# The second projection's weights and the samples' operands prepared in small steps, one or two between the products of a part

## The chip, the core and the metric

The kernel runs on one core of a Trainium2 chip. The core has a matrix engine (TensorE, PE in the profile), a vector engine (VectorE, DVE), a scalar engine (ScalarE, ACT), a general engine (GpSimd, POOL) and a sequencer that issues most of the transfers (SyncE, SP); 16 DMA engines carry them. The metric is the time of one execution on the device in microseconds (us), the median of several runs.

## The reference, cut to what matters

The kernel computes one layer of a streaming encoder: a recurrent and an attention mixer, a cross-attention into a memory, and a feed-forward block, for 1024 prompt rows and for 128 sample rows (8 requests of 16). Only the last product and the norm behind it are touched:

```python
def swiglu(x, w_in, w_out):
    g, u = jnp.split(x @ w_in, 2, axis=-1)
    return (jax.nn.silu(g) * u) @ w_out              # w_out: 2816 x 1024, the "second projection"
...
    x = layer_norm(ALPHA * x + swiglu(x, w_ffn_in, w_ffn_out), ln_g[2], ln_b[2])
```

## The kernel before, in words

All matrices are fp32. A product of two fp32 operands is done as three matmuls in a shorter format: each operand is split into a high part (a cast on ACT) and a low part (operand minus high part, a subtraction on DVE or POOL), and `mm3` (line 96) issues high by high, high by low and low by high into one PSUM bank. A matmul of 128x128 by 128x512 is the unit.

The second projection is the last stage, `second_projection`. The 2816 rows of its weights are 22 blocks of 128, taken as 11 *pairs*; each pair, with the two halves of the 1024 columns, is a 2x2 block matrix (a11, a12, a21, a22). A Strassen-like scheme needs seven block products (*steps*) rather than eight; its weight operands are A11, S1, S2, S4, S3, A12, A22 with s1 = a21+a22, s2 = s1−a11, s4 = a12−s2, s3 = a11−a21, and its activation operands B11, T1, T2, B22, T3, B21, T4 come from `h_scratch` in DRAM. The table `steps` lists for each step the PSUM bank (x, z or w, two buffers each), the weight operand, the activation operand and where its result goes.

`PARTS` cuts the 11 pairs into (0,2), (2,4), (4,6), (6,8), (8,11). For each part the seven steps run for row blocks b = 0 and 1, then the samples' product of the part (bank s), then the seven steps for b = 2 and 3. In the first four parts a step of a turn has 12 matmuls, 6 for each b. In the last part there are three pairs and each b runs alone, 9 matmuls a step; its results go through `final_norm` (lines 1083 to 1097), the layer norm: statistics and two multiplies on DVE, `rs` (a power) and two more operations on POOL, one on ACT, and then the stores. The norm of the samples (`ys`) was issued between b = 1 and b = 2.

After a step's matmuls for one b, DVE adds the bank into the accumulator `y` (line 1196; bank w instead is copied by ACT to `tap` and added by POOL, line 1194). Steps S2, S3 and A22 go on accumulating in bank x, and S4 in bank z, so such a step's matmuls wait for the DVE add of the step before in that bank.

`prepare(i)` makes the operands of pair i: two loads of 512 KB into `raw2` (line 1108, SP), four sums on POOL (lines 1111 to 1114), eight casts on ACT (line 1121), six low parts on DVE and two, A21 and A22, on POOL (line 1122). It takes one of 14 buffers ("units") of pool `c` for the sums, four for the results and, for every other pair, one for raw2; the other raw2 is in pool `f2`. `operand()` gives a step its activation operand, loads (line 1164, `hq`) three steps ahead and splits (lines 1173 and 1174, `hh` and `hl`) one step ahead. The order of instructions on each engine comes from a scheduler which starts from the order in which the code issues the work; engines run their own lists in order and wait on semaphores.

Pairs 0 and 1 are prepared in the stage before, and the scheduler moves pair 2 there too. The others are prepared as `more()` is called in the code: one pair of the next part between the first half and the sample's product, the rest after the sample's product; pair 3 is so prepared in part 0.

Of the kernel before, what the change touches and what calls it, by code (L numbers as in the profile page):

```python
# [9 lines left out]
F32 = mybir.dt.float32  # L10
F32R = mybir.dt.float32r
# [3 lines left out]
ALU = mybir.AluOpType  # L15
# [3 lines left out]
P = 128  # L19
# [13 lines left out]
PAIRS = FT // 2  # L33
# [19 lines left out]
class Order:  # L53
# [49 lines left out]
def trunk(ctx, tc, I, O):  # L103
    nc = tc.nc
# [814 lines left out]
    def unit(c, name, dt=F32):  # L919
        return c.tile([P, 2048], dt, name=name, tag="u", bufs=14)  # L920
# [178 lines left out]
    def second_weights(c):  # L1099

        prepared = {}

        def prepare(i, at):

            raw = (at.tile([P, 2, 1024], F32, name="raw2") if at else unit(c, "raw2").rearrange("p (n x) -> p n x", n=2))
            a11, a12, a21, a22 = (raw[:, n, x * 512:x * 512 + 512] for n in range(2) for x in range(2))
            for n in range(2):
                nc.sync.dma_start(out=raw[:, n], in_=I["w_f2"][n, i])
            sums = unit(c, "s2").rearrange("p (n x) -> p n x", x=512)
            s1, s2, s3, s4 = (sums[:, n] for n in range(4))  # L1110
            G.tensor_tensor(s1, a21, a22, op=ALU.add)  # L1111
            G.tensor_tensor(s2, s1, a11, op=ALU.subtract)
            G.tensor_tensor(s4, a12, s2, op=ALU.subtract)
            G.tensor_tensor(s3, a11, a21, op=ALU.subtract)
            out = {}
            for both in ((("A11", a11), ("S1", s1)), (("S2", s2), ("S4", s4)), (("S3", s3), ("A12", a12)),
                         (("A22", a22), ("A21", a21))):
                t = unit(c, "w2", F32R).rearrange("p (n x) -> p n x", x=512)
                for n, (name, src) in enumerate(both):
                    hi, lo = t[:, 2 * n], t[:, 2 * n + 1]  # L1120
                    S.copy(hi, src)  # L1121
                    (G if name in ("A21", "A22") else V).tensor_tensor(lo, src, hi.bitcast(F32), op=ALU.subtract)  # L1122
                    out[name] = hi, lo
            prepared[i] = out
# [12 lines left out]

        return prepared, prepare, first_operands

    def second_projection(f2, c, ahead, prepared, prepare):  # L1140

        y = {}
        sums = [bank("s") for _ in range(2)]
        gb = []
# [54 lines left out]
            if bn is not None:  # L1199
                V.bn_stats(bn[:, half], y[b, e][:, hs])  # L1200

        def blocks(part, bs, gb):

            ws = [prepared[i] for i in range(*part)]
            bk = {}
            bn = {(b, e): sm.tile([P, 2, 6], F32, name="bn", bufs=6) for b in bs for e in range(2)} if gb else {}
            for which, w, h, start, (e, half, fin) in steps:
                for b, hs in zip(bs, ahead.pop((bs[0] + part[0], h), None) or operand()):
                    if start:
                        bk[which, b] = bank(which)  # L1210
                    ps = bk[which, b]
                    for n, wk in enumerate(ws):
                        mm3(ps, hs[n], wk[w], start and n == 0, n == len(ws) - 1, skip_group_check=not start)
                    add(b, e, half, ps, None if fin is None else bn.get((b, fin)), which)
                    if gb and (w == "S3" or w == "A22"):
                        final_norm(y[b, fin], gb, bn[b, fin], b, fin)
                    yield

        def sample_operands(part):
            out = []  # L1220
            for i in range(*part):
                q, hi, lo = (f2.tile([P, 2, P], t, name=x, bufs=2) for x, t in (("hs", F32), ("hsh", F32R), ("hsl", F32R)))
                nc.sync.dma_start(out=q, in_=hs_dram[:, i])
                split(q, hi, lo)
                out.append((hi, lo))
            return out

        def sample(part, hs, first, last):
            ws = [prepared[i] for i in range(*part)]
# [16 lines left out]
        for n, part in enumerate(PARTS):  # L1246
            last = n == len(PARTS) - 1
            if n == 0:
                for e in range(2):
                    for b in range(2):  # L1250
                        nc.sync.dma_start(out=y[b, e], in_=x2_dram[TILES[b + 4 * e]])
            if last:
                both = unit(c, "ln_gb").rearrange("p (n x) -> p n x", n=2)
                gb = [both[:, n] for n in range(2)]
                for n in range(2):
                    nc.sync.dma_start(out=gb[n], in_=I["ln"][4 + n:5 + n, :].broadcast_to([P, D]))
            for bs in ((0,), (1,)) if last else ((0, 1),):
# [24 lines left out]
            yield from blocks(part, (2, 3), gb)  # L1282

    def feed_forward(rows):
        right.close()
        c = ctx.enter_context(tc.tile_pool(name="c", bufs=1, side="right", reuse_waits="tile"))
        ops = {o: tuple(unit(c, f"{o}_{x}", F32R).rearrange("p (k x) -> p k x", k=4) for x in "hl") for o in OPS}
        ready, filled = Event(), Event()
        order.add(all_operands(ops, rows, ready), 6)
        order.add(filler(filled), 10)  # L1290
        yield ready
        yield filled
        prepared, prepare, first_operands = second_weights(c)
        ops2 = {}

        def ahead():
            for i in range(PARTS[0][1]):
                prepare(i, None)
# [193 lines left out]
```

## Time and profile before

| | |
|---|---|
| runs, us | 1694.09 median of 3 (1692.74 to 1698.1) |
| profiled execution, us | 1695.47, its span 1693.6 |
| PE busy | 1618.2 us, 96% of the span |
| DVE, ACT, POOL busy | 1127.7, 677.5, 497.1 us |
| the stage of the change | first y load issued at 1397.6, last instruction 1690.0, end 1693.6 |
| its transfers, from 1395 us on | 40.6 MB |

A PE that is busy is not at its peak; what counts in this stage are the places where PE has nothing to do, or is granted half its clock (PEclk 0.5). One step of 12 matmuls takes 2.81 us when nothing holds it, 0.234 us for each.

### The profile page before, as it was taken

To read this page: it belongs to the slowest core of one execution; us is meant where nothing else is said; L and a number is where in the kernel's file an instruction comes from. 1 tells how busy PE (TensorE), PEld (TensorE's weight loads), DVE (VectorE), ACT (ScalarE), POOL (GpSimd) and SP (SyncE) were. 2 spreads that over 40 slices of the span, in tenths; PEclk is the share of its full clock that TensorE was granted. 3 is DMA by queue.
4 is the path that set the end of the run, shared out by engine and by line. 5 is a ranking of instruction groups with operands and counts; after the bars stand their busy time and mean duration, and the time that the engine had idled before them with its cause. 6 is when DMAs were issued, how large, how long until landed. Compare 5 with 4: busy or idle time off the path is not lost.

```text
span 1693.6 us, 24454 instructions
## 1 busy us (share of the span) xinstructions
PE 1618.2 (96%) x9065; PEld 1392.1 (82%) x9065; DVE 1127.7 (67%) x2025; ACT 677.5 (40%) x1372; POOL 497.1 (29%) x384
## 2 busy tenths in 40 slices
PE   8999999999999999999997999999999997889897
PEld 7998999999888987789895888888888875667675
DVE  6786688778478666787677555444444575675677
ACT  4543556446443545134343333223222343344332
POOL 1111121111000000000056443333332463765665
PEclk9999999999999999999998999999999998999999
DMA  7443343334885589637363222222222137434242
GB/s 242 140 162 123 103 148 104 100 116 127 289 280 170 174 270 307 216 115 258 125 196 104 93 100 93 97 90 97 97 96 97 69 106 245 132 104 137 90 155 87
DMA packets 118951, 247.92 MB, mean 146 GB/s; under 512 B 11952, under 2 KB 63536, under 8 KB 118832
## 3 DMA queue, kind: packets, MB, share of 16 engines
q1 hardware_dynamic: 118832, 246.36, 43.7%
q8 instruction: 71, 1.16, 0.3%
q14 instruction: 48, 0.39, 0.1%
HBM read 203.65 MB, written 42.60 MB: 145 GB/s over the span
## 4 chain that ended last, share of the span: by engine, by line
PE 78%; DVE 7%; DMA 5%; POOL 5%; issue 3%; ACT 2%; SPq 1%; POOLq 0%; ACTq 0%; DVEq 0%
PE a L96 47%; PE b L96 20%; PE x L96 4%; PE b L100 2%; PE z L96 2%; PE s L96 1%; PE w L96 1%; DMA raw<-in_w_f_dram 1%; DMA w_raw<-in_w_f_dram 1%; DVE w L1122 1%; POOL s L1111 1%; DMA w_raw<-in_w_mv_dram 1%; DVE w_lo L137 1%; ACT w L1121 1%; DVE y L1196 1%
## 5 line engine op out<-in xcount | busy, mean ns | idle before, releaser
L137 DVE TENSOR_TENSOR w_lo<-w_raw,w_hi 128x1024 fp32r<-128x1024 f32 (+1 forms) x169 | 205.2, 1217 | 116.7 <-ACT w_hi L136 116.2
L136 ACT CAST w_hi<-w_raw 128x1024 fp32r<-128x1024 f32 (+1 forms) x169 | 174.6, 1035 | 207.2 <-PE a L96 79.6
L96 PE MATMUL a<-w_hi,q_hi 128*128 128x256 f32 (+1 forms) x576 | 196.9, 343 | 0.7 <-ACT kv_sb L270 0.7
L96 PE MATMUL a<-w_lo,q_hi 128*128 128x256 f32 (+1 forms) x576 | 196.5, 341 | 0.0
L96 PE MATMUL a<-w_hi,q_lo 128*128 128x256 f32 (+1 forms) x576 | 195.5, 339 | 0.0
L96 PE MATMUL a<-q_hi,w_hi 128*128 128x384 f32 x528 | 187.0, 354 | 6.7 <-ACT q_hi L136 4.3
L96 PE MATMUL a<-q_hi,w_lo 128*128 128x384 f32 x528 | 180.1, 341 | 0.0
L96 PE MATMUL a<-q_lo,w_hi 128*128 128x384 f32 x528 | 180.0, 341 | 0.0
L96 PE MATMUL x<-w,hh 128*128 128x512 f32 x344 | 112.0, 408 | 31.5 <-DVE y L1196 15.7
L137 DVE TENSOR_TENSOR w_lo<-a,w_hi 128x1024 fp32r<-128x1024 f32 x43 | 73.0, 1698 | 78.5 <-ACT w_hi L136 78.5
L96 PEld LDWEIGHTS a<-w_hi,q_hi 128*128 128x128 f32 x576 | 108.4, 188 | 14.9 <-ACT kv_sb L270 1.1
L96 PEld LDWEIGHTS a<-w_lo,q_hi 128*128 128x128 f32 x576 | 108.6, 189 | 14.2 <-issue 1.2
L96 PEld LDWEIGHTS a<-w_hi,q_lo 128*128 128x128 f32 x576 | 108.4, 188 | 12.5 <-issue 0.4
L96 PEld LDWEIGHTS a<-q_hi,w_hi 128*128 128x128 f32 x528 | 100.6, 191 | 11.9 <-ACT q_hi L136 4.7
L96 PEld LDWEIGHTS x<-w,hh 128*128 128x128 f32 x344 | 65.8, 194 | 51.2 <-ACT hh L1173 16.1
L699 POOL TENSOR_TENSOR rs<-rs,mhalf 128x1 f32<-128x1 f32 x18 | 17.3, 959 | 303.5 <-DVE rs L698 303.5
L96 PE MATMUL a<-T_h,w_hi 128*128 128x512 f32 x264 | 104.7, 396 | 0.0
L96 PE MATMUL a<-T_h,w_lo 128*128 128x512 f32 x264 | 104.6, 396 | 0.0
L96 PE MATMUL a<-T_l,w_hi 128*128 128x512 f32 x264 | 104.6, 396 | 0.0
L96 PEld LDWEIGHTS a<-q_lo,w_hi 128*128 128x128 f32 x528 | 100.8, 191 | 1.9 <-DVE q_lo L137 0.9
L96 PEld LDWEIGHTS a<-q_hi,w_lo 128*128 128x128 f32 x528 | 100.5, 190 | 0.8 <-DVE w_lo L137 0.4
L1173 ACT CAST hh<-hq 128x512 fp32r<-128x512 f32 (+1 forms) x82 | 47.0, 582 | 91.5 <-PE x L96 46.2
(308 smaller groups left out, 3929.9 us busy)
## 6 DMA issues: line engine op xcount, KB each, us to landing
a<-in_w_f_dram SPq DMA_DIRECT2D x44, 512.0 KB, 5.1
w_raw<-in_w_fm_dram SPq DMA_DIRECT2D x41, 512.0 KB, 3.9
h_scratch<-w_raw SPq DMA_DIRECT2D x55, 256.0 KB, 2.2
hq<-h_scratch SPq DMA_DIRECT2D x54, 256.0 KB, 3.9
w_raw<-in_w_tm_dram SPq DMA_DIRECT2D x24, 512.0 KB, 3.4
w_raw<-in_w_out_dram SPq DMA_DIRECT2D x24, 512.0 KB, 5.1
w_raw<-in_w_mq_dram SPq DMA_DIRECT2D x24, 512.0 KB, 4.3
w_raw<-in_w_mo_dram SPq DMA_DIRECT2D x24, 512.0 KB, 4.5
```

Of the source, the lines that this page charges most:

```text
L96: return self.eng.matmul(out, lhsT, rhs, **kw)
L100: return self.eng.transpose(out, in_, identity)
L136: S.copy(hi, src)
L137: V.tensor_tensor(lo, src, hi.bitcast(F32), op=ALU.subtract)
L699: G.tensor_tensor(rs, rs, mhalf[:, 0:1], op=ALU.pow)
L1111: G.tensor_tensor(s1, a21, a22, op=ALU.add)
L1121: S.copy(hi, src)
L1122: (G if name in ("A21", "A22") else V).tensor_tensor(lo, src, hi.bitcast(F32), op=ALU.subtract)
L1173: S.copy(hi, q)
L1196: V.scalar_tensor_tensor(y[b, e][:, hs], y[b, e][:, hs], 1.0 if key in y else ALPHA, ps, op0=ALU.mult, op1=ALU.add)
```

## The change

`prepare` no longer issues anything. It returns a table of small steps: `load`, two `a` (two sums each), four `u` (two casts each) and four `l` (two low parts each). A new function `plans` puts the steps of the next part's pairs, and the loading (`load_sample`) and splitting (`part_sample`) of the samples' operands, into lists, one list for each of the seven steps of the first half and of the second half; `blocks` runs a list after its step. The first of the next part's pairs is planned into the first half, the second (and third) into the second half; the second's load also stands in the first half. The samples' operands get three buffers instead of two. `more()` is gone, and so is the preparation of one pair ahead after the first half: pair 3 is now loaded in part 0, before the second step's operands.

```diff
-            raw = (at.tile([P, 2, 1024], F32, name="raw2") if at else unit(c, "raw2")...)
...
+            raw, sums, units, out = [], [], [], prepared.setdefault(i, {})
+
+            def load():
+                t = at().tile([P, 2, 1024], F32, name="raw2") if at else unit(c, "raw2").rearrange("p (n x) -> p n x", n=2)
+                for n in range(2):
+                    nc.sync.dma_start(out=t[:, n], in_=I["w_f2"][n, i])
...
+            def add(k):
...
+            def upper(k):
...
+                    S.copy(t[:, 2 * n], src)
+
+            def lower(k):
...
+                    (G if name in ("A21", "A22") else V).tensor_tensor(lo, src, hi.bitcast(F32), op=ALU.subtract)
+                    out[name] = hi, lo
+            return {"load": load, **{f"a{k}": (lambda k=k: add(k)) for k in range(2)},
+                    **{f"u{k}": (lambda k=k: upper(k)) for k in range(4)},
+                    **{f"l{k}": (lambda k=k: lower(k)) for k in range(4)}}
...
-        def blocks(part, bs, gb):
+        def blocks(part, bs, gb, plan=()):
...
+                for x in plan[z] if plan else ():
+                    x()
...
-        def more():
-            i = len(prepared)
-            if i < PAIRS:
-                prepare(i, f2 if i % 2 else None)
+        def plans(n, load_sample, part_sample):
+            first, second = [[] for _ in steps], [[] for _ in steps]
+            first[2].append(load_sample)
+            first[5].append(part_sample)
+            if n + 1 < len(PARTS):
+                nexts = [prepare(i, (lambda: f2) if k == 1 else None) for k, i in enumerate(range(*PARTS[n + 1]))]
...
+                put(first, 0, load=0, a0=1, a1=2, u0=2, l0=3, u1=3, l1=4, u2=4, l2=5, u3=5, l3=6)
+                put(first, 1, load=1)
+                put(second, 1, a0=0, a1=0, u0=0, l0=1, u1=1, l1=2, u2=2, l2=3, u3=3, l3=4)
+                if len(nexts) > 2:
+                    put(second, 2, load=3, a0=5, a1=5, u0=5, l0=6, u1=6, l1=6, u2=6, l2=6, u3=6, l3=6)
+            return first, second
...
                 for n in range(2):
                     nc.sync.dma_start(out=gb[n], in_=I["ln"][4 + n:5 + n, :].broadcast_to([P, D]))
+            load_sample, part_sample, hx = sample_operands(part)
+            first, second = plans(n, load_sample, part_sample)
             for bs in ((0,), (1,)) if last else ((0, 1),):
-                yield from blocks(part, bs, gb)
-            hs = sample_operands(part)
+                yield from blocks(part, bs, gb, first if bs[-1] == 1 else ())
...
-            while len(prepared) < min(part[1] + 1, PAIRS):
-                more()
-            yield from sample(part, hs, n == 0, last)
+            yield from sample(part, hx, n == 0, last)
...
-            while len(prepared) < PARTS[n + 1][1]:
-                more()
-            yield from blocks(part, (2, 3), gb)
+            yield from blocks(part, (2, 3), gb, second)
```

One thing the diff does not say aloud: in the last part the loop over `gb` uses the name `n` too and leaves it at 1, so that `plans(n, ...)` there is `plans(1, ...)`. It plans the pairs of `PARTS[2]` once more; the list `first` then runs with block b = 1 of the last part. Pair 4 is prepared a second time in full (two loads, four sums, eight casts, eight low parts) and pair 5 is loaded a second time; nothing reads what they make.

How the instructions stand now, at three places.

SP at the start of the stage: the loads of `y` (the accumulators of b = 0 and 1), then those of `hq` (activation operands from the third step on). Before:

```order
L1251 DMA y_13037<-x2_scratch 128x1024
L1251 DMA y_13040<-x2_scratch 128x1024
L1251 DMA y_13041<-x2_scratch 128x1024
L1164 DMA hq_13080<-h_scratch 128x512
L1164 DMA hq_13082<-h_scratch 128x512
```

and in the changed kernel:

```order
L1295 DMA y_13037<-x2_scratch 128x1024
L1295 DMA y_13040<-x2_scratch 128x1024
L1295 DMA y_13041<-x2_scratch 128x1024
L1110 DMA raw2_13086<-in_w_f2_dram 128x1024 x2
L1184 DMA hq_13089<-h_scratch 128x512
L1184 DMA hq_13091<-h_scratch 128x512
```

Pair 3's two loads (raw2_13086), which stood behind eight `hq` and more, now stand ahead of the first; on ACT two casts of this pair stand ahead of the first `hh`, on POOL its four sums ahead of the first `hl`, and on DVE two of its low parts ahead of the first `hl`.

DVE where part 0 ends and part 1 begins: y_13038 and y_13039 take the last step of b = 2 and 3, y_13036 and y_13037 the first of part 1; raw2, s2 and w2 are here the loaded blocks, the sums and the results of pair 4, the first of part 1. Before:

```order
L1174 TENSOR_TENSOR hl_13489<-hq_13442,hh_13488 128x512
L1196 SCALAR_TENSOR_TENSOR y_13038<-y_13038,x_13298 128x512
L1122 TENSOR_TENSOR w2_13612<-raw2_13604,w2_13612 128x512
L1122 TENSOR_TENSOR w2_13612<-s2_13607,w2_13612 128x512
L1196 SCALAR_TENSOR_TENSOR y_13039<-y_13039,x_13306 128x512
L1122 TENSOR_TENSOR w2_13617<-s2_13607,w2_13617 128x512
L1196 SCALAR_TENSOR_TENSOR y_13036<-y_13036,x_13448 128x512
L1122 TENSOR_TENSOR w2_13617<-s2_13607,w2_13617 128x512
L1196 SCALAR_TENSOR_TENSOR y_13037<-y_13037,x_13456 128x512
```

and in the changed kernel:

```order
L1139 TENSOR_TENSOR w2_13521<-raw2_13464,w2_13521 128x512
L1194 TENSOR_TENSOR hl_13498<-hq_13442,hh_13497 128x512
L1216 SCALAR_TENSOR_TENSOR y_13038<-y_13038,x_13273 128x512
L1139 TENSOR_TENSOR w2_13521<-s2_13489,w2_13521 128x512
L1139 TENSOR_TENSOR w2_13546<-s2_13489,w2_13546 128x512
L1216 SCALAR_TENSOR_TENSOR y_13039<-y_13039,x_13281 128x512
L1139 TENSOR_TENSOR w2_13546<-s2_13489,w2_13546 128x512
L1216 SCALAR_TENSOR_TENSOR y_13036<-y_13036,x_13448 128x512
L1139 TENSOR_TENSOR w2_13571<-s2_13489,w2_13571 128x512
L1216 SCALAR_TENSOR_TENSOR y_13037<-y_13037,x_13456 128x512
```

The A11 low part moved ahead of the add of b = 2, and S2's moved ahead of the add of b = 3, beside S1's; the loads of pair 4, on SP, now stand together (before: one of pair 5, one of pair 4, two `hq`, the other of pair 4).

DVE in the last block, b = 3, of the last part: y_13039 and y_13043 are its accumulators, y_13038 and y_13042 those of b = 2, ys those of the samples; x, z, w and s are the banks. Before:

```order
L1196 SCALAR_TENSOR_TENSOR y_13039<-y_13039,x_15179 128x512
L1083 BN_AGGR mv_15157<-bn_15022 128x2
L1174 TENSOR_TENSOR hl_15241<-hq_15207,hh_15240 128x384
L1084 TENSOR_SCALAR rs_15158<-mv_15157 128x1
L1089 SCALAR_TENSOR_TENSOR y_13038<-y_13038,mv_15157,ln_gb_14646 128x512
L1086 SCALAR_TENSOR_TENSOR nb_15159<-mv_15157,rs_15158 128x1
L1196 SCALAR_TENSOR_TENSOR y_13043<-y_13043,z_15196 128x512
L1090 SCALAR_TENSOR_TENSOR y_13038<-y_13038,rs_15158,ln_gb_14646 128x512
L1196 SCALAR_TENSOR_TENSOR y_13043<-y_13043,x_15179 128x512
L1196 SCALAR_TENSOR_TENSOR y_13043<-y_13043,z_15196 128x512
```

and in the changed kernel:

```order
L1216 SCALAR_TENSOR_TENSOR y_13039<-y_13039,x_15210 128x512
L1194 TENSOR_TENSOR hl_15272<-hq_15238,hh_15271 128x384
L1139 TENSOR_TENSOR w2_14867<-raw2_14817,w2_14867 128x512
L1139 TENSOR_TENSOR w2_14867<-s2_14837,w2_14867 128x512
L1139 TENSOR_TENSOR w2_14889<-s2_14837,w2_14889 128x512 x2
L1139 TENSOR_TENSOR w2_14925<-s2_14837,w2_14925 128x512
L1139 TENSOR_TENSOR w2_14925<-raw2_14817,w2_14925 128x512
L1216 SCALAR_TENSOR_TENSOR y_13043<-y_13043,z_15227 128x512
L1216 SCALAR_TENSOR_TENSOR y_13043<-y_13043,x_15210 128x512
L1216 SCALAR_TENSOR_TENSOR y_13039<-y_13039,w_15304 128x512
L1316 SCALAR_TENSOR_TENSOR ys_15032<-ys_15032,s_13034 128x512
L1316 SCALAR_TENSOR_TENSOR ys_15032<-ys_15032,s_13035 128x512
```

The second preparation's six low parts now stand between the adds of b = 3, and behind them the samples' sums and norm and the norm of b = 2, which stood before b = 3's adds or between them; the last three adds of b = 3 and its two norms come behind those. The load of `ys` on SP takes the buffer of the second preparation's sums (s2_14837), and so comes after the low parts that read them; those sums and results take buffers that the S1 step of b = 3 is the last to read.

More of the change, by code (lines that the diff above doesn't have):

```diff
@@ L1103, in prepare @@
         def prepare(i, at):
[L1105 to L1111, printed above, removed]
@@ new lines, in load @@
+            def load():
+                t = at().tile([P, 2, 1024], F32, name="raw2") if at else unit(c, "raw2").rearrange("p (n x) -> p n x", n=2)
+                for n in range(2):
+                    nc.sync.dma_start(out=t[:, n], in_=I["w_f2"][n, i])
+                raw.extend(t[:, n, x * 512:x * 512 + 512] for n in range(2) for x in range(2))
+            def add(k):
+                a11, a12, a21, a22 = raw
+                if k == 0:
+                    t = unit(c, "s2").rearrange("p (n x) -> p n x", x=512)
+                    sums.extend(t[:, n] for n in range(4))
+                s1, s2, s3, s4 = sums
+                for o, x, y, op in (((s1, a21, a22, ALU.add), (s2, s1, a11, ALU.subtract)),
+                                    ((s4, a12, s2, ALU.subtract), (s3, a11, a21, ALU.subtract)))[k]:
+                    G.tensor_tensor(o, x, y, op=op)
@@ new lines, in names @@
+            def names(k):
+                a11, a12, a21, a22 = raw
+                s1, s2, s3, s4 = sums
+                return ((("A11", a11), ("S1", s1)), (("S2", s2), ("S4", s4)), (("S3", s3), ("A12", a12)),
+                        (("A22", a22), ("A21", a21)))[k]
+            def upper(k):
+                t = unit(c, "w2", F32R).rearrange("p (n x) -> p n x", x=512)
+                units.append(t)
+                for n, (_, src) in enumerate(names(k)):
+                    S.copy(t[:, 2 * n], src)
@@ L1120, in prepare @@
+            def lower(k):
+                t = units[k]
+                for n, (name, src) in enumerate(names(k)):
                     hi, lo = t[:, 2 * n], t[:, 2 * n + 1]
-                    S.copy(hi, src)
                     (G if name in ("A21", "A22") else V).tensor_tensor(lo, src, hi.bitcast(F32), op=ALU.subtract)
                     out[name] = hi, lo
-            prepared[i] = out
+            return {"load": load, **{f"a{k}": (lambda k=k: add(k)) for k in range(2)},
+                    **{f"u{k}": (lambda k=k: upper(k)) for k in range(4)},
+                    **{f"l{k}": (lambda k=k: lower(k)) for k in range(4)}}
@@ L1206, in blocks @@
             bn = {(b, e): sm.tile([P, 2, 6], F32, name="bn", bufs=6) for b in bs for e in range(2)} if gb else {}
-            for which, w, h, start, (e, half, fin) in steps:
+            for z, (which, w, h, start, (e, half, fin)) in enumerate(steps):
                 for b, hs in zip(bs, ahead.pop((bs[0] + part[0], h), None) or operand()):
@@ L1217, in blocks, with load, parts @@
                     yield
+                for x in plan[z] if plan else ():
+                    x()
         def sample_operands(part):
[L1220 to L1226, printed above, removed]
+            raw, out = [], []
+            def load():
+                for i in range(*part):
+                    raw.append(f2.tile([P, 2, P], F32, name="hs", bufs=3))
+                    nc.sync.dma_start(out=raw[-1], in_=hs_dram[:, i])
+            def parts():
+                for q in raw:
+                    hi, lo = (f2.tile([P, 2, P], F32R, name=x, bufs=3) for x in ("hsh", "hsl"))
+                    split(q, hi, lo)
+                    out.append((hi, lo))
+            return load, parts, out
         def sample(part, hs, first, last):
@@ L1297, in ahead @@
             for i in range(PARTS[0][1]):
-                prepare(i, None)
+                steps = prepare(i, None)
+                for x in ("load", "a0", "a1", "u0", "l0", "u1", "l1", "u2", "l2", "u3", "l3"):
+                    steps[x]()
             ops2.update(first_operands())
```

10 lines of the change are left out of this document (3 added, 7 removed).

## The prediction

> **What bounds the kernel now.** I read the page's head and its chain first, then the waits of PE from 1395 us on, then the chain and the windows at each place where PE waits, because PE has 96% of the span and a change in this stage can win only where it stands still.
>
> ```profile
> span 1693.6 us, 24454 instructions
> PE 78%; DVE 7%; DMA 5%; POOL 5%; issue 3%; ACT 2%; SPq 1%; POOLq 0%; ACTq 0%; DVEq 0%
> ...
> PE x L96 <- DVE y L1196: 15.7, 8, 4.1
> PE x L96 <- ACT hh L1173: 15.6, 1, 15.6
> PE z L96 <- DVE y L1196: 5.1, 5, 1.5
> ```
>
> In the waits the columns are total us, times, longest. PE waits in this stage for two things: once 15.6 us at the start, for the first activation operand, and 13 times, 20.8 us in all, for DVE to add a bank into y so that the bank can be written again. Where these adds are late is seen in the windows around the four changes of part (busy time of PE, PEld, DVE, ACT and POOL with the number of instructions, then PEclk, the DMA engines' share and GB/s).
>
> ```profile
> 1453.10:1471.30 18.20, 14.88 (x56) 11.29 (x55) 14.57 (x18) 7.99 (x15) 17.07 (x12) 0.91 0.13 35
> 1503.40:1523.20 19.80, 14.38 (x56) 9.91 (x56) 15.84 (x18) 7.93 (x15) 18.68 (x13) 1.00 0.15 47
> 1555.30:1574.00 18.70, 14.94 (x56) 11.31 (x55) 14.62 (x18) 8.04 (x15) 17.56 (x12) 0.91 0.16 50
> 1604.40:1618.00 13.60, 9.48 (x32) 7.20 (x31) 9.47 (x12) 5.87 (x12) 11.32 (x9) 0.75 0.29 90
> ...
> 1476.92 5.62 PE s L96 x24
> ```
>
> 24 matmuls in 5.62 us give 0.234 us each. 56 of them need 13.1 us, so the first three windows hold 5.1, 6.7 and 5.6 us too much, 17.4 together; 32 need 7.5, so the fourth holds 6.1. In all of them POOL is busy 83 to 94%: it makes the next pairs' sums there, and casts, low parts and adds queue behind it.
>
> **The change, part by part.** The sum is made against the profiled execution, 1695.47 us, which is 1.4 above the median of 1694.09; what comes out is added to the median.
>
> *Start.* The chain and one window:
>
> ```profile
> 1400.90 7.05 DMA hq<-h_scratch
> 1407.97 0.63 ACT hh L1173
> 1408.64 4.93 PE x L96 x12
> ...
> 1401.50:1408.00 6.50, 0.00 (x0) 0.00 (x0) 2.29 (x4) 0.03 (x1) 0.00 (x0) 0.50 1.01 384
> ```
>
> The DMA engines are full (share 1.01, 384 GB/s) until hq lands and PE starts. Pair 3's 1.05 MB now stand ahead of hq: 1.05 MB / 384 GB/s = 2.7 us. Then, on ACT, the S1 cast of pair 3 stands ahead of the first hh and waits for POOL's first sum (1.3 by the row at 1601.81 below): raw2 in at about 1410.0, sum 1411.3, cast 1411.9, hh 1412.6; DVE's S1 low part (1.1) stands ahead of hl, which comes at about 1413.7, one or two matmuls late. So +4 to +5; I take +4.5, bounds +2.7 (transfers alone) and +6 (all sums on POOL late too). What this buys is that pair 3 is ready early.
>
> *Inside part 0.* DVE made four low parts of pair 3 in a row ahead of an add:
>
> ```profile
> 1437.62 3.50 DVE w L1122 x4
> 1441.12 0.61 DVE y L1196
> 1441.77 1.67 PE z L96 x6
> ```
>
> Now they alternate with the adds; this wait goes: −1.4 (bounds 0 and −1.7; two low parts remain ahead of an add somewhere).
>
> *The changes of part 0 to 1, 1 to 2, 2 to 3.* Two rows of SP's list (issue times), then the chain, at 1 to 2:
>
> ```profile
> 1494.91 0.81 SPq L1108 DMA_DIRECT2D raw<-in_w_f_dram  x2
> 1496.72 0.52 SPq L1108 DMA_DIRECT2D raw<-in_w_f_dram  x1
> ...
> 1502.81 1.30 POOL s L1111
> 1504.13 0.63 ACT w L1121
> 1504.78 1.09 DVE w L1122
> 1505.87 0.61 DVE y L1196
> 1506.52 1.68 PE x L96 x6
> ...
> L1111 POOL TENSOR_TENSOR s<-raw 128x512 f32<-128x512 f32 x8 | 11.7, 1461 | 12.6 <-DMA raw<-in_w_f_dram 12.6
> ```
>
> Sum, cast, low part, add, matmul: the sum starts when the second half of the first new pair lands (POOL's idle time ahead of such sums, 12.6 us, is all put down to this load), issued at 1496.72, after a half of the other pair and two hq. Now both halves of this pair are issued together from 1494.9 on, with nothing of the other pair ahead: 1.4 us from the issue and, at 384 GB/s, 1.3 from the 512 KB no longer ahead, 2.7 together. POOL's work in the window is not less, so the window shrinks by what POOL starts earlier, and by a little more since the low parts are not bunched any more. Against it, S2's low part (1.09) now stands ahead of the add of b = 3 beside S1's, so the first wait hardly shrinks; the gain comes at the second and third. I take 3 for each, −9; bounds 0 (the earlier sums only fill POOL's queue, which has a tap and an hl in it) and −14 (all but 1.1 us of each window). The other pair's loads go ahead of later hq; a step's hq is loaded three steps ahead, 8.4 us, so this is hidden, and if that cover goes, hh is late next.
>
> *The change 3 to 4.*
>
> ```profile
> 1601.81 1.29 POOL s L1111
> 1603.10 1.70 POOL s L1114
> 1604.80 1.68 POOL s L1112
> 1608.99 4.18 PE x L96 x9
> ...
> 1609.00:1611.50 2.50, 2.50 (x6) 2.02 (x7) 1.44 (x2) 2.09 (x5) 1.62 (x2) 0.50 0.00 0
> ```
>
> PE waited until 1608.99 since two low parts (S1, S2), behind three sums, stood ahead of the add of b = 2, and then ran at half clock. Now S1's alone stands there, and S2's and others ahead of a later add: −1.7 (bounds 0 and −4.5).
>
> A rule bears on the tail below. The longest wait (4.1 us) is followed by PEclk 0.50 for over 2.5 us, while at 1503.4 to 1523.2 the clock stays at 1.00 behind the wait that ends at 1506.52. The Trainium skill, in "TensorE: Matmul & The Clock Gate", "What's actually happening", says that the array falls to half rate after an idle window of about 3.4 us and needs about as long a busy time to come back; these two rows agree with it. By it the two long waits that I expect in the last block would each leave 9 to 18 matmuls at half rate; I count none of it, and by the rule the sum would be up to 2 us higher.
>
> *The last part, up to its last block.* The samples' norm leaves the place between b = 1 and b = 2: −0.5 (bounds 0 and −1). Two MB of loads that nobody reads are added in part 4, beside work that waits little for DMA; 0, bounds 0 and +2.
>
> *The last block.* This is the second preparation of pair 4. Its sums and results need buffers that S1 of b = 3 reads last, so none of it can start earlier. Let t be the end of that S1, 1670.46 by the row of its last matmuls; from there the kernel before took 1693.6 − 1670.5 = 23.1 us.
>
> ```profile
> 1670.23 0.39 PE L96 MATMUL z<-w,hl 128*128 128x512 f32 x1
> 1673.99 2.34 PE z L96 x9
> 1679.20 0.71 DVE bn L1200
> 1680.41 1.00 POOL rs L1085
> 1686.50 0.82 ACT y L1088
> 1687.39 1.26 POOL y L1091
> 1688.69 1.30 POOLq L1473
> ...
> L1090 DVE SCALAR_TENSOR_TENSOR y<-y,rs,ln_gb 128x512 f32<-128x512 f32 x8 | 6.0, 745 | 0.0
> ys<-x_scratch SPq DMA_DIRECT2D x1, 512.0 KB, 5.7
> ...
> 1650.00:1694.00 44.00, 31.09 (x131) 24.13 (x129) 31.26 (x56) 8.59 (x14) 24.49 (x21) 0.91 0.26 90
> ```
>
> 1. POOL's four sums, the first just before t, 1.3 to 1.7 each: the last at t+4.9. Casts and low parts trail it (0.63 and 1.09): the sums are read to the end at t+7.1, DVE is through at t+7.8. The adds of b = 3 stand behind the low parts: PE's S4, at 1673.99 = t+3.5 before, starts at about t+8.5.
> 2. The ys load is issued at t+7.2 since it takes the buffer of the sums. It took 5.7 before, among other loads; with little beside it now I take 4.4, so t+11.6. DVE stands at the ys sums until then, with the add of S3 and the last one behind.
> 3. From there the five norms (ys, two of b = 2, two of b = 3) run on POOL one behind the other, where three were out of the way before. Two sums and four bn (0.7 each) and small ones: first rs at t+16.0, done 17.0; nb and ACT to 18.0; POOL twice 1.3 for ys, 20.6, and for the first of b = 2, 23.2; then three times rs, nb, ACT and twice 1.3 (1.0 + 0.2 + 0.8 + 2.6 = 4.6): 37.0. DVE's multiplies (0.745) and adds between make it later by some 2: 38.7.
> 4. The end came 3.6 us after the last POOL operation (1690.0, from the row at 1688.69): t+42.3.
>
> 42.3 − 23.1 = +19. Bounds: +15 (no DVE piece between, ys in at t+9.1) and +23 (ys lands in 5.7, half clock, POOL slowed beside DVE).
>
> Sum: 4.5 − 1.4 − 9 − 1.7 − 0.5 + 19 = +10.9. 1694.1 + 11 = 1705.
>
> **The rivals.**
> - *The boundaries keep their waits.* POOL is 94% busy there, and if it is bound by its work and not by the landing, the −9 and −0.5 are nothing: 4.5 − 1.4 − 1.7 + 19 = +20, 1714. For it speaks POOL's share, and S2's low part ahead of the add; against it the 12.6 us that POOL idles for the landing.
> - *The boundaries lose nearly all.* −16 of the 17.4: +4, 1698. For it speaks that outside the windows POOL and DVE have room; against it the same POOL share.
> - *The second preparation is hidden* (the other side). DVE is busy 31.3 of the last 44 us and POOL 24.5, room for six low parts and four sums; if they and the ys load fill holes, the 19 are gone and the sum is −8: 1686, faster. It decides where the tail costs less than about 3 us; between 3 and 13 the kernel is the same. Against it: the buffers free at t, and each engine's list is in order, with ys behind the low parts and the adds behind ys.
>
> **How the numbers follow.** Forecast 0.66, waits kept 0.16, nearly all lost 0.08, hidden in full 0.06, hidden in part 0.04. A measurement tells about 0.3%, 5 us, from no change: 1689 to 1699. Faster 0.06 (hidden in full); same 0.13 (hidden in part, nearly all lost, a sliver of the forecast); slower 0.81. The start and the tail alone span +17.7 to +29, the gains 0 to −21; the range from 1697 to 1714 leaves out the hidden cases and half of the two at its ends, under 2 in 10. The likeliest case's own range is 1699 to 1711.
>
> **What would show it.** In the profile after: PE's start wait about 20 us rather than 15.6, and PE starting some 4.5 us later; the waits of PE for DVE's add fewer around the changes of part, the window from the end of a part to S3 some 3 us shorter, POOL's first sum there starting before 1500 less the shift; no group of four low parts in the chain of part 0; raw2 loads of 13 pairs; in the last block a wait of PE of about 4 to 5 us ahead of S4 and of about 10 ahead of A22, DVE waiting for the ys load, and some 42 us between the end of its S1 and the end of the span. The prediction is wrong if the time from that S1 to the end is under 35 us, if PE's start moves by less than 2, or if the three windows do not shrink, or shrink by more than 4 each.

## The result and the profile after

The changed kernel takes 1711.52 us (median of 4 runs, 1709.24 to 1713.28) against 1693.94 of the kernel before: a ratio of 1.0099 with a 95% interval of 1.008 to 1.0118, 17.6 us slower by the medians. The profiled execution took 1709.89 us, its span 1707.8, 14.2 longer than that of before. One execution of experiment 9 below ran at a granted clock of 0.648 throughout and took 2275.18 us; its median is that of the other four.

PE's waits of the changed kernel, from 1395 us on (total us, times, longest):

```profile
span 1707.8 us, 24483 instructions
...
PE x L96 <- ACT hh L1193: 19.4, 1, 19.4
PE x L96 <- DVE y L1216: 14.4, 8, 4.2
PE x L96 <- DVE rs L1084: 7.6, 1, 7.6
PE z L96 <- DVE y L1216: 5.3, 2, 4.0
PE x L96 <- DVE hl L1194: 1.1, 1, 1.1
```

The wait at the start has grown from 15.6 to 19.4 us, with one of 1.1 behind it. The waits for adds are nearly as long as before in all, 19.7 us rather than 20.8, but 4.0 of them now stand in one wait of the last block. One of 7.6 us, ahead of the very last step, is new. Where that adds up is read from the start of the same step in both traces (the A12 step, bank w, and for the last block the end of S1):

| place | before, us | after, us | lag | step by step | forecast |
|---|---|---|---|---|---|
| part 0, first half | 1419.04 | 1422.91 | +3.9 | start +3.9 | +4.5 |
| part 0, second half | 1446.09 | 1448.22 | +2.1 | −1.7 | −1.4 |
| part 1 | 1471.14 | 1471.49 | +0.4 | −1.8 | −3 |
| part 2 | 1523.00 | 1521.77 | −1.2 | −1.6 | −3 |
| part 3 | 1573.79 | 1569.86 | −3.9 | −2.7 | −3 |
| part 4, b = 0 | 1621.94 | 1618.79 | −3.2 | +0.8 | −1.7 |
| last block, end of S1 | 1670.46 | 1666.69 | −3.8 | −0.6 | −0.5 |
| end of the span | 1693.6 | 1707.8 | +14.2 | last block +18.0 | +19 |

The start in the chain that ended last:

```profile
1399.03 7.81 DMA raw<-in_w_f_dram
1406.91 0.63 ACT w L1133
1407.56 0.70 DVE w L1139
1408.28 1.27 POOL s L1121
1409.57 0.62 ACT w L1133
1410.18 1.05 ACT hh L1193 x2
1411.24 1.76 DVE hl L1194
...
1413.04 4.41 PE x L96 x10
```

Where hq and one cast stood before, pair 3's load, its first sum and its casts stand now. The first hq was issued at 1400.96 and had landed 7.8 us later, at 1408.8, but its cast `hh` starts only at 1410.18, behind the cast of pair 3 that waits for the sum. The low part `hl` is late too: PE issues two matmuls and waits 1.1 us for it.

A change of part, 1 to 2, from the chain, and PE's two waits there (in brackets the idle time ahead and what ended it); the last line is PE's first wait there in the kernel before:

```profile
1493.85 4.89 DMA raw<-in_w_f_dram
...
1498.81 3.00 POOL s L1121 x2
1501.80 1.68 POOL y L1214
1503.48 1.71 POOL s L1121
1505.21 0.63 ACT w L1133
1505.86 1.21 DVE w L1139
1507.07 0.61 DVE y L1216
...
1503.09 0.71 PE L96 MATMUL x<-w,hh 128*128 128x512 f32 x2 [0.52 <-DVE y L1216]
1507.72 0.74 PE L96 MATMUL x<-w,hh 128*128 128x512 f32 x2 [2.75 <-DVE y L1216]
...
1506.52 0.73 PE L96 MATMUL x<-w,hh 128*128 128x512 f32 x2 [2.65 <-DVE y L1196]
```

The first sum starts at 1498.81, 4.0 us earlier than before; but behind it stand a second sum, a tap and S2's sum on POOL, and S2's low part stands on DVE ahead of the add that PE waits for. The first wait nearly goes (0.5 rather than 2.65) and two later ones of before go too (0.75 and 1.65), but one of 2.75 in the second place is new.

The change 3 to 4 and the last block, again from the chain, with PE's two waits of the last block:

```profile
1606.17 0.67 DVE y L1216
1606.84 3.34 DVE w L1139 x2
1610.18 0.61 DVE y L1216
...
1665.53 4.97 POOL s L1121 x3
1670.58 1.28 POOL s L1121
...
1672.53 1.30 DVE w L1139 x2
1673.91 3.29 DMA ys<-x_scratch
...
1677.30 1.28 DVE ys L1316 x2
...
1681.17 0.99 POOL rs L1085
...
1689.80 0.97 POOL rs L1085
...
1702.84 1.30 POOLq L1515
...
1675.08 1.22 PE L96 MATMUL z<-w,hh 128*128 128x512 f32 x2 [4.02 <-DVE y L1216]
1689.34 1.19 PE L96 MATMUL x<-w,hh 128*128 128x512 f32 x2 [7.63 <-DVE rs L1084]
```

From the end of S1 (1666.69) to the end are 41.1 us, where before there were 23.1: the second preparation's sums and low parts, the ys load behind them, and the norms one behind another on POOL. From 1665.5 on no matmul stands in this chain: PE's two long waits are a sign of the late work and not what sets the end. (The wait of 7.6 us is put down to `rs`; the add that frees the bank for A22 stands on DVE just ahead of that `rs`.)

### The profile page after: what moved, and what is told of

The parts are those of the page before. It is cut to its first block, busy times and chain, and to the rows that moved or that the text cites. A ratio compares the mean times of both kernels' runs of the same rounds, so it can differ in the third digit from the quotient of the medians.

```text
span 1707.8 us, 24483 instructions
## 1 busy us (share of the span) xinstructions
PE 1618.2 (95%) x9065; PEld 1394.2 (82%) x9065; DVE 1147.4 (67%) x2031; ACT 681.7 (40%) x1380; POOL 507.5 (30%) x390
## 4 chain that ended last, share of the span: by engine, by line
PE 80%; DVE 7%; POOL 5%; DMA 4%; ACT 2%; issue 1%; SPq 0%; POOLq 0%; ACTq 0%; DVEq 0%
PE a L96 47%; PE b L96 20%; PE x L96 5%; PE z L96 3%; POOL s L1121 3%; PE b L100 2%; PE s L96 2%; DMA raw<-in_w_f_dram 2%; DVE w L1139 1%; PE w L96 1%; DMA w_raw<-in_w_f_dram 1%; DMA w_raw<-in_w_mv_dram 1%; ACT w L1133 1%; DVE T_l L940 1%; DVE w_lo L137 1%
## 5 line engine op out<-in xcount | busy, mean ns | idle before, releaser
L96 PE MATMUL x<-w,hh 128*128 128x512 f32 x344 | 113.7, 413 | 41.5 <-ACT hh L1193 19.4
L96 PEld LDWEIGHTS a<-w_hi,q_hi 128*128 128x128 f32 x576 | 108.3, 188 | 14.5 <-ACT kv_sb L270 1.1
```

The source lines that it names most:

```text
L96: return self.eng.matmul(out, lhsT, rhs, **kw)
```

## The experiments

All ratios are to the kernel before, run on the same chip beside them.

| kernel | median, us | ratio, 95% interval | profiled span, us | of it from PE's first long wait on, us | end of S1 of the last block to the end, us |
|---|---|---|---|---|---|
| before | 1694 to 1695 | 1 | 1693.6 | 300.6 | 23.1 |
| changed | 1711.52 | 1.0099, 1.008 to 1.0118 | 1707.8 | 316.4 | 41.1 |
| 1: changed, one preparation | 1693.93 | 0.9993, 0.9983 to 1.0003 | 1692.0 | 299.1 | 23.2 |
| 2: before, second preparation | 1716.22 | 1.0124, 1.0107 to 1.014 | 1714.0 | 320.8 | 40.9 |
| 3: 1 and pair 3 late | 1690.21 | 0.9972, 0.9962 to 0.9982 | 1686.3 | 292.0 | 23.0 |
| 4: 3 and low parts behind adds | 1684.84 | 0.9939, 0.9922 to 0.9956 | 1685.2 | 289.1 | |
| 5: 4 and third pair earlier | 1678.58 | 0.9897, 0.9878 to 0.9915 | 1675.1 | 286.9 | |
| 6: 5 and hq before y | 1682.47 | 0.9922, 0.9908 to 0.9936 | 1677.7 | 285.9 | |
| 7: changed, ys in another buffer | 1709.85 | 1.0074, 1.0054 to 1.0093 | 1701.8 | 311.9 | 36.4 |
| 8: 6 and samples held | 1676.41 | 0.9885, 0.9865 to 0.9905 | 1670.5 | 281.0 | 23.5 |
| 9: 8 and sums behind taps | 1675.90 | 0.9889, 0.9872 to 0.9906 | | | |

Runs of one kernel differ by up to 9 us, and the end of the stage ahead lies up to 5 us to either side of before's in one profiled execution; medians are compared with medians, and inside a profile the waits and the steps from place to place. The fifth column counts from the start of PE's wait for the first activation operand and so leaves the stage ahead out.

**1. One preparation.**

```diff
-                for n in range(2):
-                    nc.sync.dma_start(out=gb[n], in_=I["ln"][4 + n:5 + n, :]...)
+                for g in range(2):
+                    nc.sync.dma_start(out=gb[g], in_=I["ln"][4 + g:5 + g, :]...)
```

> The changed kernel with the loop over the norm's rows under another name, so that the last part plans nothing and pair 4 is not prepared a second time; nothing else differs. Theory (the second preparation costs what the tail lost): all is as in the changed kernel up to the end of S1 of the last block, 3.8 us ahead of before, and from there to the end 23 us as before, not 41: about 1690 us, 4 below before. Rival (the norms are late because the plans moved the samples' operands or the norms themselves, not because of the second preparation): the last stretch stays over 33 us and the time at 1702 to 1712.

The last stretch is back at 23.2 us, PE's wait ahead of S4 at 1.25, and the time at that of before; the forecast of about 1690 was 4 us too low, since the lead ahead of the last block is 1.7 us here and not 3.8.

```profile
1672.32 0.71 PE L96 MATMUL z<-w,hh 128*128 128x512 f32 x2 [1.25 <-DVE y L1216]
```

The name of one loop variable is worth 17 us; what the change does otherwise comes to nothing measurable. Its gains and losses are all there: in its profile the first three changes of part win 2.1, 3.6 and 2.6 us and the inside of part 0 1.7, the change 3 to 4 loses 2.1, the start loses 6.3.

**2. The second preparation alone, in the kernel before.**

```diff
                 yield from blocks(part, bs, gb)
+            if last:
+                prepare(4, None)
+                raw = f2.tile([P, 2, 1024], F32, name="raw2")
+                for g in range(2):
+                    nc.sync.dma_start(out=raw[:, g], in_=I["w_f2"][g, 5])
```

> The kernel before, and only a second preparation of pair 4 and a second load of pair 5 added behind block b = 1 of the last part, read by nobody. Theory: it alone costs what the tail of the changed kernel lost: +18 us (15 to 21), about 1712, with 38 to 44 us from the end of S1 of the last block to the end. Rival (hidden: the engines have room for it in this part): within 3 us of before, 1694 to 1697.

+21 us, at the upper edge of the forecast, and the two waits of the last block are those of the changed kernel to within 0.2 us:

```profile
1681.51 1.22 PE L96 MATMUL z<-w,hh 128*128 128x512 f32 x2 [4.01 <-DVE y L1196]
1695.81 1.19 PE L96 MATMUL x<-w,hh 128*128 128x512 f32 x2 [7.42 <-DVE rs L1084]
```

With the first experiment this shows it from both sides. 18 of the 21 are the last stretch (40.9 against 23.1); in the profile 2.9 more are lost at the changes 2 to 3 (1.1) and 3 to 4 (1.8, with a wait of 5.49 us rather than 4.12). Why they are lost there isn't shown; experiment 1 has a wait of 5.42 at 3 to 4 as well.

**3. Pair 3 late.**

```diff
-                put(first, 1, load=1)
+                put(first, 1, load=6 if n == 0 else 1)
```

> As the kernel with one preparation, and in part 0 the load of pair 3 planned behind the last step of the first half instead of the second step, so that it no longer stands ahead of the first activation operands. Theory (the 3.9 us at the start are pair 3's 1 MB and its casts and low parts in the queues ahead): PE starts the third step at 1408.6 as before, -3.9; of the 1.7 us won inside part 0 up to 1.7 are lost again: 1686 to 1688. Rival (the start is late for another reason, such as what the stage before leaves): no change against the kernel with one preparation, 1690.

PE's start wait is 15.0 us and the third step starts within 0.7 us of before. 3.7 us less than experiment 1 by the medians, as the theory said; the time itself, 1690.2, is the number that the rival gave, but only because experiment 1 came at 1693.9 and not at 1690. What was won inside part 0 stays (−1.7), which the expectation gave up. The run moves the load together with all that hangs on it, and doesn't tell the bytes from the cast.

```profile
PE x L96 <- ACT hh L1193: 15.0, 1, 15.0
```

**4. Low parts behind the adds.** The scheduler's freedom is cut for DVE: nothing of a planned step may be issued ahead of the last add that the code has before it.

```diff
-                V.scalar_tensor_tensor(y[b, e][:, hs], ...)
+                latest["V"] = V.scalar_tensor_tensor(y[b, e][:, hs], ...)
...
                 for x in plan[z] if plan else ():
-                    x()
+                    with tc.issue_after(latest["V"].ins):
+                        x()
```

> As the kernel with pair 3 late, and every planned step's DVE instructions are held behind the last DVE add that the code issued before them, so that no low part of a later pair can stand ahead of an add that the code has earlier. Theory (the waits at the four changes of part, 14.4 us in the changed kernel, are low parts that the scheduler moved ahead of adds, not a lack of engine time): 10 to 14 us less than the kernel with pair 3 late, 1673 to 1677. Rival 1 (POOL's work is the bound there): the waits come back at other places, for weights or operands, and the time is within 3 us of it, 1684 to 1690. Rival 2 (the third pair of the last part, planned behind the last two steps, comes too late): the first three changes win 8 to 10 us and the last one loses 3 to 6: 1679 to 1684.

5.4 us less than experiment 3, half of the theory. The time, 1684.84, lies just above rival 2's range and at the lower end of rival 1's, which was counted from a base some 3 us lower. PE's waits from the end of part 0 to the start of part 4 fall from 14.4 us (eight) to 9.4 (six), and one of these is new, for a low part of the third pair:

```profile
1599.56 0.51 PE L96 MATMUL x<-w,hh 128*128 128x512 f32 x1 [3.47 <-DVE w L1139]
```

At the first three changes the waits fall from 8.9 to 5.9 us, by the order on DVE alone. At the change 3 to 4 the wait for adds goes and that for a low part stands in its place: this much of rival 1 is borne out. In the last part PE waits 2.3 us ahead of an S4 rather than 1.3, and two waits of 1.4 and 0.6 us are new. So the order was worth some 5 us by the medians (2.9 by the profiles, from PE's first long wait on), and 2.6 us of wait remain at the change 0 to 1.

**5. The third pair earlier**, and the samples' splits not held.

```diff
-                    put(second, 2, load=3, a0=5, a1=5, u0=5, l0=6, ...)
+                    put(second, 2, load=3, a0=4, a1=5, u0=5, l0=5, ...)
...
+                    if x.__name__ in ("load", "parts"):
+                        x()
+                        continue
```

> As the kernel with the low parts held behind the adds, but the third pair of the last part gets its first sums, casts and low parts one step earlier in the plan (its A11 and S1 low parts behind step S3's adds, no longer behind those of the last step), and the samples' operands are not held. Theory (PE's 3.5 us wait for a low part at the change 3 to 4 is the plan's place for that pair, and the 2.2 us lost in the last part are the samples' low parts held back): 4 to 6 us less, 1679 to 1681. Rival (that pair's buffers come free only with the last steps of part 3, so that an earlier place in the plan changes nothing): within 1.5 us of it, 1683 to 1686.

6.3 us less by the medians, 2.3 by the profiles from PE's first long wait on. The 3.47 and the loss in the last part are gone, so the buffers were no obstacle; but PE waits there for an add (1.88) and, what is new, for an activation operand, ahead of A12 (2.65). The two edits of this run were not made apart, so how much each is worth isn't shown.

**6. The first hq before two of the y loads.**

```diff
             for e in range(2):
                 for b in range(2):
                     nc.sync.dma_start(out=y[b, e], ...)
+                load(0)
```

> As the kernel with the third pair earlier, and the first hq load stands on SP behind the first two y loads instead of all four. Theory (PE's first wait of 14 to 15 us ends when the first hq lands, and what lands ahead of it is what counts, as with pair 3's 1 MB): 1.05 MB less ahead at some 400 GB/s, -2.6 us against the kernel with the third pair earlier, PE's first wait 11 to 12.5 us. Rival (the two y loads that now come later hold back the adds of S1, and with them step S4, or the wait has another end): the first wait shrinks but S4 waits as long, no change.

The wait shrank as forecast, by 2.7 us (13.1 to 10.4), but the median is 3.9 us higher. The two intervals touch (0.9915 and 0.9908), and from PE's first long wait on the profile is 1.0 us shorter than that of 5: 3.2 won up to part 0's first A12 step, 3.6 lost at the change 0 to 1, 1.4 won behind it. Where the 3.9 of the medians come from is so not shown; what the start won was lost at the change 0 to 1, where both waits became 2.7 us (1.6 and 1.3 in 5) and the granted clock fell to 0.50 behind the second. DVE there, between two pairs of adds:

```profile
1443.15 1.27 DVE L1217 SCALAR_TENSOR_TENSOR y<-y,x 128x512 f32<-128x512 f32 x2
1444.35 1.82 DVE L1195 TENSOR_TENSOR hl<-hq,hh 128x512 fp32r<-128x512 f32 x1
1446.09 1.50 DVE L137 TENSOR_TENSOR hsl<-hs,hsh 128x256 fp32r<-128x256 f32 x1
1447.52 1.75 DVE L1195 TENSOR_TENSOR hl<-hq,hh 128x512 fp32r<-128x512 f32 x1
1449.19 1.27 DVE L1217 SCALAR_TENSOR_TENSOR y<-y,x 128x512 f32<-128x512 f32 x2
```

A low part of the samples, not needed before the samples' product, and two of the activations stand ahead of the second pair.

**8. The samples held** there too (all parts but the last), on top of 6.

```diff
-                    if x.__name__ in ("load", "parts"):
+                    if x.__name__ == "load" or (x.__name__ == "parts" and gb):
```

> As the kernel with hq before y, but the samples' splits are held behind the code's adds as well, in all parts except the last. Theory (that kernel's start is 2.7 us earlier but it loses 4 us at the change 0 to 1, since the samples' low parts, ready there, stand ahead of the add of b = 3): its second wait of 2.7 us there shrinks by 1 or more and the slow clock behind it goes, 2 to 3 us less, 1679 to 1681. Rival (the wait is made by the activation operands' low parts, slowed to 1.75 us beside POOL's sums): within 1 us of it, 1681 to 1684.

6 us less than 6 by the medians, 4.9 by the profiles, more than expected: the hsl row is gone, the waits are 0.4 and 1.3 us rather than 2.7 each, and full clock holds behind them. The activations' low parts are as slow as before (3.53 us for two), and a wait of 1.3 us is left behind them: the rival holds for that part.

```profile
1438.10 1.27 DVE L1217 SCALAR_TENSOR_TENSOR y<-y,x 128x512 f32<-128x512 f32 x2
1439.30 3.53 DVE L1195 TENSOR_TENSOR hl<-hq,hh 128x512 fp32r<-128x512 f32 x2
1442.75 1.27 DVE L1217 SCALAR_TENSOR_TENSOR y<-y,x 128x512 f32<-128x512 f32 x2
...
1443.48 0.73 PE L96 MATMUL x<-w,hh 128*128 128x512 f32 x2 [1.28 <-DVE y L1217]
```

This kernel takes 1676.4 us, 1.2% below before, and is the fastest of all with experiment 9.

**7. ys in a buffer that is free early**, the second preparation as in the changed kernel.

```diff
-                ys = unit(c, "ys")[:, :1024]
+                ys = f2.tile([P, 2, 1024], F32, name="raw2")[:, 0]
```

> The changed kernel with the second preparation as it is, but ys takes the buffer of the second load of pair 5, which is free early, instead of that of the second preparation's sums; so the samples' norm and that of b = 2 stand ahead of the six low parts, as before. Theory (of the 18 us in the last block the larger part is the late ys load with five norms behind one another on POOL, the smaller the six low parts ahead of the add that S4 waits for): S4 still waits about 4 us, the wait of 7.6 us ahead of A22 is gone, from the end of S1 of the last block to the end 28 to 32 us instead of 41: 1698 to 1702. Rival (the low parts and sums alone cost it): over 38 us, 1708 to 1712.

The last stretch takes 36.4 us, between theory and rival and nearer the rival, in whose range the time lies (1709.85). So the late ys and the pile of norms account for 4.7 of the 18 with this order, and 13.3 are left with ys early. The wait ahead of A22 shrinks as expected, to 0.9, but that of S4 grows from 4 to 10 us, since the norm of the block b = 2 is now between the sums on POOL and behind the low parts on DVE, ahead of S4's add:

```profile
1670.57 0.09 POOL rs L1085
...
1671.50 1.57 POOL s L1121
...
1674.68 1.76 DVE w L1139 x2
...
1677.58 1.76 DVE y L1090
1679.34 0.61 DVE y L1216
...
1679.99 4.21 PE z L96 x9
```

The two parts are not additive: whichever comes first holds back the other.

**9. POOL's sums behind the taps**, on top of 8.

```diff
-                    with tc.issue_after(latest["V"].ins):
+                    for k in latest: held.enter_context(tc.issue_after(latest[k].ins))
...
+                latest["G"] = G.tensor_tensor(y[b, e][:, hs], y[b, e][:, hs], t, op=ALU.add)
```

> As the kernel with the samples held, and the planned POOL work (sums, A22 and A21 low parts) is held behind the last tap addition that the code issued before it, so that no sum runs while the last steps of a part and their low parts are on DVE. Theory (the two waits at the change 0 to 1, 2.7 us each, come from DVE operations that take 1.2 to 1.8 us beside POOL's sums and 0.7 without): both shrink to under 1 us, 3 to 5 us less than the kernel with the samples held, 1675 to 1678. Rival (POOL is then late with the sums, and the waits come back one or two steps later, for low parts): within 2 us of it.

No difference from 8, as the rival said. The theory had little left to win: the two waits of 2.7 us that it names are those of experiment 6, and in 8 they were 0.4 and 1.3. There is no profile of this kernel to set beside the others, so whether the sums' cost moved elsewhere stays open.

## Why the prediction was right

The forecast was 1705 us, range 1697 to 1714; measured 1711.5, which is 0.5 above the likeliest case's own range (1699 to 1711). The mechanism of the likeliest case came, and its largest term, the second preparation in the last block, was nearly exact; two of the gains that should have offset it were too large.

- *Last block, +19*: +18.0. S4 starts at t+8.4 (said 8.5), the ys load is issued at t+7.2 (7.2), lands after 3.3 us (4.4 taken), the first rs starts at t+14.5 (16.0), the last POOL operation ends at t+37.4 (38.7). PE's waits ahead of S4 and A22 are 4.0 and 7.6 (said 4 to 5, and about 10). Experiments 1 and 2 show that the second preparation is the cause; how it splits into late ys and late low parts experiment 7 shows only in part.
- *Start, +4.5*: PE starts the fourth step 3.9 us later; counted from the end of the matmuls ahead of the wait, which came 1.6 us earlier in this execution, 5.5. The parts are as said: counted so, the first hq landed 2.5 us later (2.7 said), its cast stood another 1.4 behind pair 3's, and the rest is the late low part (1.1) and a longer time at half clock. Experiment 3 takes it away again.
- *Inside part 0, −1.4*: −1.7.
- *The changes of part, −9*: −6.1, and −8.3 in experiment 1, whose program is the same there. The first sum did start 4 us earlier. The term was mis-sized where it says that the first wait hardly shrinks and the gain comes behind it: it is the other way round, the first wait falls to 0.3 to 1.2 us and the second is made anew by S2's low part, 1.4 or 2.75 us long. Against the forecast the waits did not become fewer: with the change 3 to 4 they are eight before and eight after, 16.2 and 14.4 us. Part of the gain is the clock, which the term did not count: before, the granted clock fell to 0.50 behind the first wait of two of these changes (0 to 1 and 2 to 3), in the changed kernel behind a wait of one (1 to 2), in experiment 1 behind none.
- *The change 3 to 4, −1.7*: +0.8 (+2.1 in experiment 1). This step failed: the low parts that left the place ahead of the first add stand ahead of the second (3.34 us for two), and PE's wait of 4.2 us only moved, with one of 1.3 ahead of it. Order was only part of it: with the low parts held behind the adds that wait goes, but 3.5 us for the third pair's low part come in its place (experiment 4), or 1.9 and 2.7 for an add and an activation operand (experiment 5).
- *The samples' norm out of the way, −0.5*: −0.6.
- *The clock behind the two long waits, counted as nothing*: the first 9 matmuls behind each of them took 4.2 us rather than 2.3, at a granted clock of 0.50. These two waits, 4.0 and 7.6 us, agree with the Trainium skill's rule ("TensorE: Matmul & The Clock Gate", "What's actually happening"), to which the forecast gave up to 2 us. Nothing was the right count all the same: the chain to the end passes through POOL and not through these matmuls. The prediction also read the full clock behind the wait that ends at 1506.52 (2.65 us) as agreeing with that rule; the two windows beside it in its own table have PEclk 0.91, and there the clock fell behind waits of 2.23 and 2.67 us. More on this stands in the last section.

By the terms the span should have been 1693.6 + 10.9 = 1704.5; it is 1707.8. The 3.3 between are the smaller gains at the changes of part (2.9) and at 3 to 4 (2.5), less what the start, part 0, the samples' norm and the last block came below their terms (2.0). That the gap is no wider is partly luck: the stage ahead was 1.6 us shorter in this execution, and from PE's first long wait on the change cost 15.8 us, not 14.2. The median is 17.4 above the one shown for before, 3.2 more than the spans differ, since before's profiled execution was 1.4 above its median and this one is 1.6 below.

The rival that POOL's work is the bound at the changes of part (waits kept) had the time nearly right, 1714, but not the reason: the first three changes did win, 6.1 us, and experiment 4 takes another 3.0 us off the waits there by the order on DVE alone. At the change 3 to 4, where nothing was won, the runs don't rule it out.

## What to carry to other kernels

Read what a reordered program issues, not only its diff: rows that come twice (here 13 pairs loaded where 11 exist) point to a preparation that nobody reads, and in the last block, where no later work covers it, its cost is its whole chain. Work that is put "between" other work in the code stays there only if the scheduler has no reason to move it: here low parts went ahead of adds that matmuls waited for. Tying each planned step behind the last add before it won 5.4 us by the medians, where the plan as it stood (experiment 1) won 1.3, with an interval that reaches past nothing. At a stage's start, count what lands ahead of the first operand (2.5 of the 5.5 us lost here) and also what stands ahead of its cast and its low part on the other engines (the rest).

## What the runs showed of the hardware that was not expected

The granted clock fell behind waits much shorter than the longest one, and not each time. In the changed kernel a wait of 2.76 us (change 0 to 1) was followed by full clock, and one of 2.75 us (1 to 2) by a slow stretch:

```profile
1458.90:1463.00 4.10, 4.04 (x17) 3.30 (x18) 4.10 (x6) 2.64 (x6) 4.01 (x4) 1.00 0.19 41
1509.40:1513.50 4.10, 4.10 (x13) 3.20 (x12) 4.10 (x5) 1.04 (x3) 4.10 (x4) 0.61 0.35 77
```

PEclk (the sixth figure behind the length) is 1.00 in one and 0.61 in the other, 17 matmuls against 13 in 4.1 us. The slow stretch began some 1.5 us after PE had started again, at 1507.72. The Trainium skill, "TensorE: Matmul & The Clock Gate", "What's actually happening", names an idle window of about 3.4 us that runs freely. A wait of 2.75 us is shorter than that, so no such window fits into it and by the page neither wait should count; here the runs differ from the page. That the same wait counts once and once not would suit a window that does not start with the wait, but no run here shows what decides it. The slow stretch cost 1.5 us here: from the end of the wait to the next step in bank x, 5.6 us rather than 4.1.

Low parts on DVE took 0.7 us alone and up to 1.8 beside POOL's sums and taps (1.82 and 1.75 in experiment 6's rows, while POOL was busy throughout), so DVE's list takes longest just where POOL catches up.
